# Issuing operand loads ahead of transposes, w_down sums six products later, and the cast of x three quads later

## The chip, the cores and the metric

The kernel runs on one core of one Trainium2 chip. The metric is device time in microseconds, the median of several executions.

## The reference

```python
# x: (8, 1024, 1024), w_gate, w_up: (1024, 4096), w_down: (4096, 1024), all float32
gate = x @ w_gate
up = x @ w_up
gate = 0.5 * gate * (1 + np.tanh(np.sqrt(2 / np.pi) * (gate + 0.044715 * gate ** 3)))
h = gate * up
return (h @ w_down).astype(np.float32)
```

## The kernel before

The 8192 rows of x are worked in eight passes (0 to 7) of 1024. Each pass has a gate/up phase and a down phase (the first two matrix products of the reference, and the third). Both are written with fewer block products than the plain way (sums of blocks are formed first), in a plain form for passes 0 to 2 (gate/up) and 0 to 3 (down), and in a finer, "fast" form for the rest. The fast form needs more sums of weight blocks. Those of w_gate and w_up are made in passes 1 and 2 and kept in HBM, the chip's large memory, as `w_ops`. Those of w_down are made in eight "units", two in each of the down phases of passes 2 and 3 and of the gate/up phases of passes 3 and 4, and kept as `wd_quads`. Operands are read from HBM into SBUF, the memory that the engines read, and TensorE's products are "evicted", that is read out of its accumulators by VectorE and ScalarE.

The fast gate/up phase is 8 "quads" of 26 products, so 208 products, numbered from 0. A unit there is a load followed by 20 steps, three products apart. The step number k is used all through this text. Each step first issues the stores of what the step before made, then takes the buffer that has been free longest and makes one sum on VectorE, some steps also a copy on ScalarE:

```python
def gate_up_fast(p):
    owed = {}
    steps = {}
    if p in UNITS_UP:                                   # passes 3 and 4
        free = deque(hf["s3"][:, 4096 + j * 512 : 4608 + j * 512] for j in range(8))
        for i, u in enumerate(UNITS_UP[p]):             # two units
            load, fs = wd_unit(u, hf["s3"][:, 0:4096], free)
            steps[i * 78] = load
            for k, f in enumerate(fs):
                steps[i * 78 + 14 + 3 * k] = f
    for q in range(NQ):
        # ... extra = the steps of this quad
        if q == 2 and p + 1 < NPASS:
            extra.setdefault(3, []).append(lambda: cast_x(p + 1))
        owed = quad(p, q, owed, extra)

def cast_x(p):                                          # fp32 to fp16, HBM to HBM
    r = slice(p * TOK, (p + 1) * TOK)
    nc.gpsimd.dma_start(out=xh[r, :], in_=x2[r, :])

# in wd_unit:
def stores():
    for v, n in made:
        nc.sync.dma_start(out=wdq[...], in_=v...)       # wd_quads
        if n < 8:
            free.append(v)
    made.clear()
def step(i):
    stores()
    n, op, a, b = WD_SUMS[i]
    v = at[n] = free.popleft()
    combine(node(n), op, node(a), node(b))              # VectorE
    # ... some steps also a scaled copy on ScalarE; buffers without further use are freed
```

Eight buffers serve a unit, and some are taken again four steps, 12 products, after their store.

Stores, operand loads and transposes are all issued by one engine, SyncE, in program order. And the down phase of the plain form reads w_down in chunks through a ring in SBUF:

```python
for v, name in enumerate(DSEQ):                         # 7 products of 2 chunks
    for nb in range(2):
        kc = 2 * v + nb
        for g in range(G):
            # ... 8 matmuls on chunk kc
            if v == 0 and nb == 0 and g == 0:
                flush()
            # ... evictions; the loads of two w_down units (steps 0)
            if nb == 0 and g == 0 and p + 1 < NPASS:
                if v == (2 if p < FAST - 1 else 0):     # pass 2: in the first product
                    transpose_x(p + 1)                  # four transposes on SyncE
        # p > 0:
        if kc == 0 and p < FAST:
            for k in range(3, 6):
                load_d(p, k)                            # chunks 3 to 5
        load_d(p, kc + 6)
```

Of the kernel before, what the change touches and what calls it, by code (L numbers as in the profile page):

```python
# [173 lines left out]
def kernel(  # L174
# [20 lines left out]
    NPASS = M // TOK  # L195
# [3 lines left out]
    FAST = 3  # L199
# [47 lines left out]
    def cast_x(p):  # L247
        r = slice(p * TOK, (p + 1) * TOK)
        nc.gpsimd.dma_start(out=xh[r, :], in_=x2[r, :])

    def transpose_x(p):
        for n, kh, mh in (("b11", 0, 0), ("b21", 1, 0), ("b12", 0, 1), ("b22", 1, 1)):
            r0 = p * TOK + mh * MH
            nc.sync.dma_start_transpose(  # L254
                out=xq[n], in_=xh[r0 : r0 + MH, kh * MH : (kh + 1) * MH]
            )
# [74 lines left out]
    def load_raw(p, q):  # L331
        if q < NQ:
            for w in range(2):
                nc.gpsimd.dma_start(
                    out=raw(p, q)[:, w], in_=w_v[w][:, :, q * 512 : (q + 1) * 512]
                )
# [182 lines left out]
    def d_chunk(p, k):  # L519
        if p == 0 and k % 2:  # L520
            return half_block(k // 2)
        o = 4096 * d_place(p, k)
        return rg[:, o : o + 4096].rearrange("p (n h) -> p n h", n=8)

    def load_d(p, k):
        if p >= DFAST:
            load_q(k + 2)
        elif k < 14 and (p or k % 2 == 0):
            nc.sync.dma_start(out=d_chunk(p, k), in_=wdop[k])
# [10 lines left out]
    def load_q(c):  # L540
        if c < len(WD_ENTRIES):
            nc.sync.dma_start(out=q_chunk(c), in_=wdq[c])
# [48 lines left out]
    def flush():  # L591
        for f in pending:
            f()
        pending.clear()
# [163 lines left out]
    def load_a(c):  # L758
        if c < NQ * NCH:
            q, j = divmod(c, NCH)  # L760
            nc.sync.dma_start(
                out=a_chunk(c).rearrange("p (e n) -> p e n", e=2), in_=wop[q, j]
            )
# [81 lines left out]
# [3 lines that stand above are left out]
        if p in UNITS_UP:  # L848
            free = deque(hf["s3"][:, 4096 + j * 512 : 4608 + j * 512] for j in range(8))
            for i, u in enumerate(UNITS_UP[p]):  # L850
                load, fs = wd_unit(u, hf["s3"][:, 0:4096], free)
                steps[i * 78] = load
                for k, f in enumerate(fs):
                    steps[i * 78 + 14 + 3 * k] = f
        for q in range(NQ):
            extra = {k: [steps[q * SLOTS + k]] for k in range(SLOTS) if q * SLOTS + k in steps}
            if q == NQ - 1 and p >= DFAST:
                for c in range(2):
                    extra.setdefault(2 + c, []).append(lambda c=c: load_q(c))
            if q == 2 and p + 1 < NPASS:  # L860
                extra.setdefault(3, []).append(lambda: cast_x(p + 1))
            owed = quad(p, q, owed, extra)
        for n in sorted(owed):
            pending.extend(owed[n])
# [11 lines left out]
    def down(p):  # L876
# [8 lines left out]
        def store(n, g, mh, hh):  # L885
            r0 = p * TOK + mh * MH + g * P
            nc.sync.dma_start(
                out=out2[r0 : r0 + P, hh * HH : (hh + 1) * HH], in_=tmp[:, t[n, g]]
            )
            tmp_free.append(t[n, g])  # L890

        def snap(n, g, b="a"):
            nc.scalar.activation(tl((n, g)), ps_all[:, bank[b, g]], COPY, scale=OSC)  # L893

        def add(n, b, g):
            o = tmp[:, t[n, g]]
            nc.vector.scalar_tensor_tensor(o, ps_all[:, bank[b, g]], OSC, o, MUL, ADD)

        def hsum(o, a, b, op, r):
            s = slice(4 * r, 4 * r + 4)  # L900
            nc.vector.tensor_tensor(hq[o][:, s, :], hq[a][:, s, :], hq[b][:, s, :], op)
# [41 lines left out]
        steps = {}  # L943
# [10 lines left out]
        for v, name in enumerate(DSEQ):  # L954
            b = CHAIN[name]
            first = name in ("P1", "P5")
            lhs = hq[D_OPERAND[name]]
            for nb in range(2):
                kc = 2 * v + nb
                dc = d_chunk(p, kc)  # L960
                for g in range(G):
                    if first and nb == 0:
                        bank[b, g] = ps_free.popleft()
                    for n in range(8):
                        j = 8 * nb + n
                        nc.tensor.matmul(  # L966
                            ps_all[:, bank[b, g]],
                            lhs[:, j, g * P : (g + 1) * P],
                            dc[:, n, :],
                            start=(first and j == 0),  # L970
                            stop=(j == NP - 1),
                            skip_group_check=True,
                        )
                    if v == 0 and nb == 0 and g == 0:
                        flush()
                    for f in todo:
                        f()
                    todo.clear()
                    if nb == 1:
                        if name == "P1":  # L980
                            bank["c", g] = ps_free.popleft()
                            nc.scalar.copy(ps_all[:, bank["c", g]], ps_all[:, bank["a", g]])
                        elif name == "P2":
                            snap("s1", g, "c")
                            ps_free.append(bank["c", g])
                            todo.append(lambda g=g: store("s1", g, 0, 0))
                        elif name == "P6":
                            snap("s2", g)
                        elif name == "P7":
                            snap("s3", g)  # L990
                            add("s3", "b", g)
                            todo.append(lambda g=g: store("s3", g, 1, 1))
                        elif name == "P3":
                            add("s2", "b", g)
                            ps_free.append(bank["b", g])
                            todo.append(lambda g=g: store("s2", g, 0, 1))
                        elif name == "P4":
                            snap("o21", g)
                            ps_free.append(bank["a", g])
                            todo.append(lambda g=g: store("o21", g, 1, 0))  # L1000
                    for s in sums.get((name, nb, g), ()):
                        hsum(*s)
                    for f in steps.get((2 * v + nb) * G + g, ()):
                        f()
                    if p == 0:
                        for f in half_work.get((kc, g), ()):
                            f()
                    if nb == 0 and g == 0 and p + 1 < NPASS:

                        if v == 0 and 0 < p < FAST - 1:  # L1010
                            cast_x(p + 1)
                        if v == (2 if p < FAST - 1 else 0):
                            transpose_x(p + 1)
                    if v >= x_from and work:
                        work.popleft()()
                if p == 0:
                    if kc == 0:
                        for k in (2, 4, 6):
                            load_d(p, k)
                    load_d(p, {0: 8, 6: 10, 8: 12}.get(kc, 14))  # L1020
                else:
                    if kc == 0 and p < FAST:
                        for k in range(3, 6):
                            load_d(p, k)
                    load_d(p, kc + 6)
                if p + 1 < FAST:
                    if kc == 10:
                        load_raw(p + 1, 0)
                elif p + 1 < NPASS and kc >= 8:
                    ahead = order[0]  # L1030
                    order[0] = ahead[2:] + ahead[:2]
                    load_a(2 * (kc - 8))
                    load_a(2 * (kc - 8) + 1)
                    order[0] = ahead
# [225 lines left out]
    for p in range(NPASS):  # L1260
        if p < FAST:
            gate_up_one(p)
        else:
            gate_up_fast(p)
        if p < DFAST:
            down(p)
        else:
            down_fast(p)
# [30 lines left out]
```

## Time and profile before

| | before |
|---|---|
| timed, three runs | 2276.72, 2282.41, 2283.21 us |
| profiled span | 2273.7 us |
| TensorE busy | 2255.4 us |
| down phase of pass 2, and of passes 0, 1 and 3 | 103.89, and 96.69 us |
| fast gate/up of pass 3, of pass 4, undisturbed (pass 6) | 183.77, 181.95, 181.65 us |

The prediction below shows the lines that these come from. How to read them: TensorE sets the time, and its share of busy time says only how little is left. The place of that little is found by timing equal phases against each other: a phase with the same matmuls that is longer than its sisters has lost the difference. The granted clock is the share of full TensorE clock in a stretch; the "sync queue" is what SyncE issues, in order.

### The profile page before, as it was taken

What the parts mean: (1) busy time and instruction counts of PE and PEld (TensorE: products, weight loads), DVE (VectorE), ACT (ScalarE), POOL (GpSimd) and SP (SyncE); (2) the same over time, 40 slices, a digit from 0 to 9 for tenths busy, and PEclk for the clock granted to TensorE, in tenths of its full rate; (3) what the DMA queues carried; (4) which work ended last, traced back from release to release, by engine and by line L of the source; (5) the groups of instructions that cost most, each with busy time, mean ns of one, the idle gap of its engine ahead of it and who ended that gap; (6) DMA issues with size and microseconds to landing.
All of it is one profiled execution on the core that took longest, in us unless ns stands there. A gap on an engine that the chain in (4) does not pass through costs nothing.

```text
span 2273.7 us, 42142 instructions
## 1 busy us (share of the span) xinstructions
PE 2255.4 (99%) x16255; PEld 1587.4 (70%) x16255; DVE 1522.1 (67%) x2170; ACT 959.7 (42%) x1876; POOL 688.1 (30%) x826
## 2 busy tenths in 40 slices
PE   9999999999999999999999999999999999999999
PEld 4444444444444445888458888888888888888888
DVE  5576368772587745876558777766776667866674
ACT  4443135651355522665226651255403553045620
POOL 1342013330133300554105450145402543034520
PEclk9999999999999999999999999999999999999999
DMA  9998959988799999998999999998989989988876
GB/s 231 180 207 209 260 144 217 228 248 261 177 214 225 267 300 317 326 381 291 263 356 334 372 331 305 332 307 287 304 315 323 322 273 322 313 315 275 283 289 229
DMA packets 305306, 632.98 MB, mean 278 GB/s; under 512 B 78992, under 2 KB 181392, under 8 KB 285840
## 3 DMA queue, kind: packets, MB, share of 16 engines
q1 hardware_dynamic: 250048, 556.88, 71.7%
q0 software_dynamic: 55056, 73.41, 19.4%
q8 instruction: 127, 2.08, 0.4%
q14 instruction: 75, 0.61, 0.1%
HBM read 565.18 MB, written 138.41 MB: 309 GB/s over the span
## 4 chain that ended last, share of the span: by engine, by line
PE 94%; DMA 3%; DVE 2%; issue 0%; SPq 0%; ACT 0%; DVEq 0%; ACTq 0%
PE ps L827 37%; PE ps L620 23%; PE ps L966 17%; PE ps L1080 16%; DMA ring<-w_ops 2%; DMA h_s<-wd_ops 1%; PE ps L1179 1%; DVE ring L349 1%; DMA h_a<-in_x_dram 0%; DMA ring<-wd_ops 0%; DVE x_sums L277 0%; SPq L254 0%; DVE tmp L639 0%; DVE h_a L657 0%; DVE h_s L410 0%
## 5 line engine op out<-in xcount | busy, mean ns | idle before, releaser
L827 PEld LDWEIGHTS <-ring 128*128 128x128 f16 x8320 | 813.6, 98 | 97.5 <-issue 2.5
L804 POOL TENSOR_TENSOR h_a<-tmp 128x256 f16<-128x256 f32 x640 | 471.8, 756 | 787.2 <-ACT tmp L792 774.4
L827 PE MATMUL ps<-x_sums,ring 128*128 128x256 f16 x5760 | 656.2, 273 | 0.3 <-DVE tmp L789 0.2
L789 DVE TENSOR_TENSOR tmp<-tmp,ps 128x512 f32<-128x512 f32 x640 | 414.3, 682 | 146.5 <-PE ps L827 102.9
L620 PEld LDWEIGHTS <-ring 128*128 128x128 f16 x2632 | 257.2, 98 | 314.0 <-issue 3.9
L774 ACT COPY tmp<-ps 128x512 f32<-128x512 f32 x520 | 303.2, 584 | 219.7 <-PE ps L827 142.0
L620 PE MATMUL ps<-x_sums,ring 128*128 128x512 f16 x1504 | 341.0, 379 | 2.2 <-DVE ring L349 1.7
L792 ACT ACTIVATE tmp<-tmp 128x256 f32<-128x256 f32 x640 | 263.2, 417 | 175.6 <-DVE tmp L787 81.6
L966 PE MATMUL ps<-ring,h_a 128*128 128x512 f16 x1408 | 307.3, 381 | 5.4 <-DMA ring<-wd_ops 5.4
L827 PE MATMUL ps<-x_b,ring 128*128 128x256 f16 x2560 | 306.0, 273 | 1.5 <-DVE tmp L789 1.3
L966 PEld LDWEIGHTS <-h_a 128*128 128x128 f16 x1536 | 150.5, 98 | 188.0 <-issue 7.9
L646 POOL TENSOR_TENSOR h_a<-tmp 128x512 f16<-128x512 f32 x94 | 150.1, 1596 | 374.8 <-ACT tmp L644 276.4
L787 DVE TENSOR_TENSOR tmp<-ps,tmp 128x512 f32<-128x512 f32 x240 | 165.3, 689 | 144.2 <-ACT tmp L774 98.8
L620 PE MATMUL ps<-x_b,ring 128*128 128x512 f16 x1128 | 259.2, 379 | 0.0
L639 DVE TENSOR_TENSOR tmp<-ps,tmp 128x512 f32<-128x512 f32 x188 | 127.0, 683 | 138.1 <-ACT tmp L631 135.3
L1080 PEld LDWEIGHTS <-h_a 128*128 128x128 f16 x1792 | 175.3, 98 | 20.4
L1080 PE MATMUL ps<-ring,h_a 128*128 128x256 f16 x1536 | 172.9, 273 | 0.0
L1137 ACT ACTIVATE tmp<-ps 128x512 f32<-128x512 f32 x48 | 28.2, 597 | 290.1 <-PE ps L1080 219.7
L631 ACT COPY tmp<-ps 128x512 f32<-128x512 f32 x188 | 109.9, 585 | 92.1 <-PE ps L620 89.5
L893 ACT ACTIVATE tmp<-ps 128x512 f32<-128x512 f32 x64 | 37.9, 596 | 240.1 <-PE ps L966 240.1
L349 DVE TENSOR_TENSOR ring<-ring 128x1024 f16<-128x1024 f16 x188 | 132.7, 720 | 5.8 <-PE ps L966 3.8
L644 ACT ACTIVATE tmp<-tmp 128x512 f32<-128x512 f32 x94 | 58.8, 626 | 146.4 <-DVE tmp L639 146.4
(94 smaller groups left out, 1552.6 us busy)
## 6 DMA issues: line engine op xcount, KB each, us to landing
ring<-w_ops SPq DMA_DIRECT2D x480, 512.0 KB, 5.2
ring<-wd_quads SPq DMA_DIRECT2D x88, 1024.0 KB, 6.2
ring<-wd_ops SPq DMA_DIRECT2D x49, 1024.0 KB, 7.2
out_dram<-tmp SPq DMA_DIRECT2D x128, 256.0 KB, 6.2
w_ops<-x_sums SPq DMA_DIRECT2D x110, 256.0 KB, 6.4
ring<-in_w_gate_dram POOLq DMA_DIRECT2D x23, 1024.0 KB, 9.2
ring<-in_w_up_dram POOLq DMA_DIRECT2D x23, 1024.0 KB, 17.9
w_ops<-h_s SPq DMA_DIRECT2D x82, 256.0 KB, 5.3
```

The lines of the kernel that those rows point to most:

```text
L349: nc.vector.tensor_tensor(o, a, b, op)
L620: nc.tensor.matmul(ps(b, w), lhs[:, k], rhs[:, k, :], start=(first and k == 0), stop=(k == KH - 1), skip_group_check=True,)
L639: nc.vector.tensor_tensor(o, ps("b", w), o, ADD)
L646: nc.gpsimd.tensor_tensor(hq[TO[n]][:, i, :], tmp[:, t[n, 1]], tmp[:, t[n, 0]], MUL)
L774: nc.scalar.copy(tmp[:, t[o[1]]], ps_all[:, bank[o[2]]])
L787: nc.vector.tensor_tensor(d, b, a, SUB)
L789: nc.vector.tensor_tensor(d, a, b, ADD if o[4] == "add" else SUB)
L792: nc.scalar.activation(d, d, GELU, scale=GSC)
L804: nc.gpsimd.tensor_tensor(h, tmp[:, t[o[1]], MQ : 2 * MQ], g, MUL)
L827: nc.tensor.matmul(ps_all[:, bank[c], w * MQ : (w + 1) * MQ], lhs[:, w, k], rhs[:, k], start=(first and w == 0 and k == 0), stop=(k == KH ...
L966: nc.tensor.matmul(ps_all[:, bank[b, g]], lhs[:, j, g * P : (g + 1) * P], dc[:, n, :], start=(first and j == 0), stop=(j == NP - 1), skip_ ...
L1080: nc.tensor.matmul(ps_all[:, bank[c], m * MQ : (m + 1) * MQ], lhs[:, j, m * P : (m + 1) * P], rhs[:, j, :], start=(first and j == 0 and m ...
```

## The change

It is meant to take two waits off TensorE's path: that of pass 2's down phase for chunk 3, by issuing chunks 3 to 5 ahead of the transposes, and those of the gate/up phases of passes 3 and 4 for a unit's load, by starting the steps later and moving the cast away from that load.

```diff
                 for k, f in enumerate(fs):
-                    steps[i * 78 + 14 + 3 * k] = f
+                    steps[i * 78 + 20 + 3 * k] = f
...
-            if q == 2 and p + 1 < NPASS:
+            if q == 5 and p + 1 < NPASS:
                 extra.setdefault(3, []).append(lambda: cast_x(p + 1))
...
                     if v == 0 and nb == 0 and g == 0:
                         flush()
+                        if p < FAST:
+                            for k in range(3, 6) if p else (2, 4, 6):
+                                load_d(p, k)
...
-                if p == 0:
-                    if kc == 0:
-                        for k in (2, 4, 6):
-                            load_d(p, k)
-                    load_d(p, {0: 8, 6: 10, 8: 12}.get(kc, 14))
-                else:
-                    if kc == 0 and p < FAST:
-                        for k in range(3, 6):
-                            load_d(p, k)
-                    load_d(p, kc + 6)
+                load_d(p, kc + 6 if p else {0: 8, 6: 10, 8: 12}.get(kc, 14))
```

## The prediction

> **What bounds the kernel now.** I read the page first (busy shares), then the chain of waits in order of time, then the time of each phase as stretches between the chain's turning points, then the sync queue's own timeline in the stretches that are too long. The page says that TensorE is busy 2255.4 of 2273.7 us, so at most 18.3 us can come from waits that end (a little more where a wait also slowed the clock), and whatever does not shorten TensorE's path is free.
>
> ```profile
> PE 2255.4 (99%) x16255; PEld 1587.4 (70%) x16255; DVE 1522.1 (67%) x2170; ACT 959.7 (42%) x1876; POOL 688.1 (30%) x826
> ```
>
> ```profile
> PE ps L966 <- DMA ring<-wd_ops: 5.4, 1, 5.4
> ```
>
> ```profile
> 795.30 13.83 PE ps L966 x64
> ...
> 814.84 6.54 DMA ring<-wd_ops
> ...
> 821.42 77.77 PE ps L966 x352
> 899.19 54.16 PE ps L827 x496
> ...
> 953.36 14.40 DMA ring<-w_ops
> ...
> 975.54 8.29 DMA h_s<-wd_ops
> ```
>
> The second line, from TensorE's waits (total, times, longest), is the largest of TensorE, a single one: in the down phase of pass 2 it stands 5.4 us for an operand chunk. The chain (start, length, what) leaves TensorE there, and again in the gate/up phases of passes 3 and 4, where it runs through slow operand loads (w_ops) into the load of a w_down unit (h_s from wd_ops).
>
> The next view sums stretches, one phase each: the down phases of passes 0, 1, 2 and 3, then the fast gate/up phases of passes 3, 4 and 6.
>
> ```profile
> 214.08:310.77 96.69, 96.69 (x449) 43.80 (x448) 46.88 (x50) 11.76 (x20) 5.67 (x5) 1.00 0.90 236
> 505.10:601.80 96.70, 96.70 (x450) 43.83 (x448) 37.10 (x43) 11.87 (x20) 4.44 (x5) 1.00 0.84 228
> 795.14:899.19 104.05, 98.65 (x451) 44.31 (x450) 53.45 (x87) 18.56 (x32) 3.41 (x4) 0.98 1.00 305
> 1082.96:1179.65 96.69, 96.69 (x450) 43.85 (x449) 55.34 (x88) 19.21 (x35) 7.37 (x8) 1.00 1.05 304
> 899.19:1082.96 183.77, 182.13 (x1665) 162.67 (x1664) 133.75 (x228) 110.75 (x242) 92.57 (x126) 1.00 0.95 332
> 1179.65:1361.60 181.95, 181.81 (x1666) 162.73 (x1665) 134.83 (x228) 110.88 (x242) 92.08 (x126) 1.00 0.98 348
> 1452.43:1634.08 181.65, 181.65 (x1666) 162.73 (x1665) 121.13 (x191) 106.31 (x229) 88.12 (x125) 1.00 0.90 308
> ```
>
> After the stretch come its length, then TensorE's busy time. The same 448 matmuls take 96.69 us in three down phases and 104.05 in pass 2: 7.36 too long. The fast gate/up takes 181.65 undisturbed, 183.77 in pass 3 (2.12 too long), 181.95 in pass 4 (0.30). These three excesses, 9.78 us, are all that the change can reach.
>
> Why the chunk was late is in the sync queue's timeline, and the stall in pass 3 in ScalarE's and TensorE's:
>
> ```profile
> 795.37 3.52 SPq L470 DMA_DIRECT2D x_sums<-wd_ops  x6
> 798.99 15.75 SPq L254 DMA_TRANSPOSE x_b<-x_half  x4
> 814.84 3.14 SPq L529 DMA_DIRECT2D ring<-wd_ops  x5
> ```
>
> ```profile
> 983.85 0.63 ACT L500 ACTIVATE h_s<-h_s 128x512 f16<-128x512 f16 x1 [3.90 <-DMA h_s<-wd_ops]
> ```
>
> ```profile
> 983.47 1.03 PE L827 MATMUL ps<-x_b,ring 128*128 128x256 f16 x8 [1.32 <-DVE tmp L789]
> ```
>
> The ring's chunks 3 to 7 were issued at 814.84, only after four transposes had held the queue for 15.75 us. TensorE had finished its first three chunks by 795.14 + 3 x 6.91 = 815.87. In pass 3 ScalarE stood 3.9 us for the unit's load. VectorE then evicted late, and TensorE waited for it.
>
> **What the Trainium skill says.** (1) "DMA: Bandwidth & Descriptors", section "Anatomy of one DMA — SWDGE (gpsimd) path": a DMA's semaphore wait is done by the issuing sequencer before dispatch, not by the DMA engines. So a DMA behind a held one in the same queue waits too; the trace agrees (15.75 us of transposes ahead of the loads). (2) Same page, "Issuing engines are not separate DMA queues": transfers of sync and gpsimd interleave on the same 16 engines. The trace agrees: after the cast of x was issued by gpsimd at 947.22, a w_ops load took 14.40 us, against a median of 5.2. (3) "TensorE: Matmul & The Clock Gate", section "What's actually happening": an array idle for about 3.4 us or more falls to half clock and needs about as long of work to come back. The trace agrees: after the 5.40 us wait the granted clock was 0.75 from 821.42 to 828, and ten matmuls took 3.95 us where they are normally 0.216 apart (96.69/448). So the wait costs 7.36 - 5.40 = 1.96 us beyond its length.
>
> **The change part by part.** It adds and removes no arithmetic: the same instructions stand on each engine, and only the sync and gpsimd queues and the places of some VectorE and ScalarE steps change.
>
> (a) Loads ahead of the transposes. In passes 0 and 1 nothing but the place in the program changes: the instruction order of the sync queue is the same there, as the transposes are issued only in the third product there. In pass 2 the three loads of chunks 3 to 5 move ahead of the six unit loads and four transposes. Their ring slots were last read by the gate/up matmuls, which end at about 795.1, so they can be issued at about 795.4 instead of 814.84. Three chunks of 1 MB at the stretch's better rate, 400 GB/s (418 right after the stall), take some 8 us: chunk 3 should land by about 801 to 803, 13 us before it is needed (815.87), chunks 4 and 5 by 807. The wait of 5.40 and the slow clock of 1.96 both go: -7.36 us.
>
> (b) Unit steps of the gate/up six products later. A product is 181.65/208 = 0.873 us, so the steps start 6 x 0.873 = 5.2 us later. In pass 3 ScalarE asked at 983.85 - 3.90 = 979.95. It will ask at 985.2, after the old landing at 983.83. That alone removes the 2.12 and the 0.30.
>
> (c) The cast in the sixth quad: 3 x 26 x 0.873 = 68 us later. In pass 3 it goes from 947 to about 1015, in pass 4 from 1228 to about 1296. That is clear of the second unit's load at product 78 (about 967), so this load no longer stands behind a blocked sync queue. It is also in time: 2 MB landed in 15.6 us, and the transposes come at 1083. Parts b and c aim at the same 2.42 us and each would nearly do alone.
>
> Sum: -7.36 - 2.42 = -9.78. From this I take back about 0.8, for the second rival below.
>
> **The rivals.** First, the queue is only reordered: chunks 6 and 7 and the stores to wd_quads stay behind the transposes, and these now start behind 3 MB more. They begin at about 803, and take 16 to 22 us (15.75 here, 22.29 in pass 3's down phase), so chunk 6 is issued at 819 to 825 and lands 7 to 10 us later, at 826 to 835. TensorE wants it at 795.14 + 6 x 6.91 = 836.6. That holds, by 2 to 10 us. If it fails, or if the late stores hold ScalarE's snapshots, a new wait on the ring of 2 to 5 us stands at the seventh chunk and the gain falls to some 4 us. Chance about one in eight.
>
> Second, the cast now meets the middle of the second unit. It comes after product 5 x 26 + 3 = 133, behind step 11 of that unit (98 + 3 x 11 = 131), where before it came after product 55, behind step 13 of the first unit (14 + 3 x 13 = 53). Stores to wd_quads issued in the next 15 us land late, and by the program's order of buffers some are wanted again four steps (10 us) after their store with VectorE waiting in order. Before, the sync queue stood for some 8 us after the cast (no issue from 954.65 to 963.00) and TensorE had no wait there, which speaks for slack. A repeat two steps earlier could cost 0 to 2 us in each of passes 3 and 4. I count 0.8 in all.
>
> Third, nothing moves: if the timed runs are ruled by something that this profile doesn't show, the gain drowns. The three timed runs spread from 2276.72 to 2283.21, while the profiled run took 2275.76. The spread of 6.5 us is nearly the size of the gain. It may be the very stalls that the change removes (they hang on the DMA's load), and then the change gives more than 9.
>
> A loss of 2% (46 us) would need TensorE idle for many times what any of these give. A gain of 2% is out of reach with 18.3 us of idle time and 2 of slow clock.
>
> **Range and chances.** 2282.4 - 9.0 = 2273.4 us, -0.4%. The profiled span should be near 2273.7 - 9.0 = 2264.7. Low end: all 9.8 won and the timed runs at the fast end of before, 2276.7 - 9.8 = 2267, less some luck: 2264. High end: 4 won from 2283.2, plus a little: 2281. The chance of faster by over 2% is 0.01, of within 2% 0.98, of slower by over 2% 0.01.
>
> **What would show it.** In pass 2 the down phase should last 96.7 us with no TensorE wait on the ring and the granted clock at 1.00 (step a); the three loads should be issued before the transposes, at about 795. The gate/up phases of passes 3 and 4 should be 181.7 to 182.5 (steps b, c), with no ScalarE wait on h_s from wd_ops. Passes 0, 1 and 5 to 7 should be unchanged. A wait of TensorE on the ring near the seventh chunk would prove the first rival, a wait on VectorE near the sixth quad of passes 3 or 4, behind a store to wd_quads, the second. If the phases shrink and the timed median doesn't, the third holds.

## More of the kernel before

"Step k's store" is the one that step k issues, of what step k - 1 made. Following the queue of free buffers by hand gives, for both units, that steps 14 to 17 write the buffers of the stores of steps 10 to 13, so step 16 that of step 12 and step 17 that of step 13: four steps, 12 products.

## The result, and the profile after

| | before | after |
|---|---|---|
| timed median (4 runs each) | 2280.80 us | 2279.63 us |
| lowest and highest | 2276.72, 2283.21 | 2276.39, 2280.80 |
| profiled span | 2273.7 us | 2274.6 us |

The ratio is 0.9994, with a 95% interval from 0.9975 to 1.0014. Ratios here are the mean time of one kernel's fast runs over that of the other's of the same rounds, so not quite the ratio of the medians. The change moved nothing that can be told from noise. The phases tell another story. First the stretches of the changed kernel: down phase of pass 2, then the fast gate/up of passes 3, 4 and 6 (stretch, its length, TensorE's busy time, then the other engines, the granted clock, the DMA's share and GB/s).

```profile
795.79:892.48 96.69, 96.69 (x450) 43.88 (x449) 53.48 (x87) 18.32 (x32) 3.42 (x4) 1.00 1.04 326
...
892.48:1079.32 186.84, 183.22 (x1666) 163.48 (x1664) 134.98 (x227) 112.61 (x242) 92.37 (x126) 0.99 0.95 328
1176.01:1362.50 186.49, 183.35 (x1667) 163.53 (x1665) 136.08 (x228) 112.54 (x242) 92.02 (x126) 0.99 0.98 338
1453.32:1634.98 181.66, 181.66 (x1667) 162.82 (x1665) 121.17 (x191) 106.32 (x229) 88.22 (x125) 1.00 0.90 308
```

Pass 2's down phase won its 103.89 - 96.69 = 7.20 us. But gate/up of pass 3 is now 186.84 - 181.65 = 5.19 us too long (2.12 before) and that of pass 4 is 4.84 too long (0.30 before): 10.03 us lost, 7.61 more than before. The gain was real, and was given back in two other phases. In pass 6, which holds no unit, the cast was moved as well and costs nothing (181.65 before, 181.66 now).

The issues of the sync queue in pass 2 (start, length, what; the count at the end) show the first part done as meant: chunks 3 to 5 go out at 795.87, and the transposes hold the queue behind them.

```profile
795.87 1.58 SPq L529 DMA_DIRECT2D ring<-wd_ops  x3
797.50 4.56 SPq L470 DMA_DIRECT2D x_sums<-wd_ops  x6
804.54 17.16 SPq L254 DMA_TRANSPOSE x_b<-x_half  x4
821.80 1.00 SPq L529 DMA_DIRECT2D ring<-wd_ops  x2
```

Now gate/up of pass 3. First the waits of TensorE in the changed kernel (total, times, longest), then the timelines of GpSimd (the cast), of the sync queue, of VectorE and of TensorE:

```profile
PE ps L827 <- DVE tmp L789: 6.8, 2, 3.6
```

```profile
1008.63 0.59 POOL L249 DMA_DIRECT2D x_half<-in_x_dram  x1
```

```profile
1009.09 0.37 SPq L481 DMA_DIRECT2D wd_quads<-h_s  x1
1011.29 2.07 SPq L761 DMA_DIRECT2D ring<-w_ops  x2
1013.45 0.38 SPq L481 DMA_DIRECT2D wd_quads<-h_s  x1
```

```profile
1024.94 0.43 DVE L277 TENSOR_TENSOR h_s<-h_s 128x512 f16<-128x512 f16 x1 [3.49 <-DMA wd_quads<-h_s]
...
1027.77 0.43 DVE L277 TENSOR_TENSOR h_s<-h_s 128x512 f16<-128x512 f16 x1 [1.20 <-DMA wd_quads<-h_s]
```

```profile
1028.84 3.31 PE L827 MATMUL ps<-x_sums,ring 128*128 128x256 f16 x16 [3.62 <-DVE tmp L789]
```

Read upwards: TensorE stood 3.62 us for an eviction of VectorE. VectorE was late because its steps 16 (at 1024.94) and 17 (at 1027.77) each waited for a store to wd_quads to read their buffer out. Step 16 waited for step 12's store, issued at 1009.09, step 17 for step 13's, issued at 1013.45. Both were issued after the cast (1008.63). The chain of waits gives the second one as 14.23 us under way, from 1013.45 to 1027.67; from 985 to 1005 such a store took a median of 5.0. The rest of the 5.19 us is the slow clock after the wait: 183.22 - 181.65 = 1.57 us of TensorE's busy time.

So the theory after the result, the "theory of the buffers", was: a store issued within the cast's 15 us lands too late for the step that takes its buffer four steps (10.5 us) later. Before, the cast stood at the same sort of place in the first unit, but steps 12 and 13 had sent their stores ahead of it. The rivals were that the sixth quad itself is a bad place; that the later steps meet TensorE's evictions badly; and that any cast in the middle of a unit holds the sync queue and so the operands.

### The profile page after: what moved, and what is told of

It is laid out like the page before. It is cut to its first block, busy times and chain, and to the rows that moved or that the text cites. A ratio compares the mean times of both kernels' runs of the same rounds, so it can differ in the third digit from the quotient of the medians.

```text
span 2274.6 us, 42143 instructions
## 1 busy us (share of the span) xinstructions
PE 2256.0 (99%) x16255; PEld 1589.0 (70%) x16255; DVE 1527.3 (67%) x2170; ACT 963.3 (42%) x1876; POOL 687.4 (30%) x826
## 4 chain that ended last, share of the span: by engine, by line
PE 95%; DVE 3%; DMA 2%; issue 1%; ACT 0%; SPq 0%; DVEq 0%; ACTq 0%
PE ps L827 39%; PE ps L620 22%; PE ps L966 17%; PE ps L1074 16%; DMA wd_quads<-h_s 1%; DVE ring L349 1%; PE ps L1173 1%; DVE tmp L639 0%; DMA h_a<-in_x_dram 0%; DVE h_a L657 0%; DVE h_s L277 0%; DVE x_sums L277 0%; DVE tmp L789 0%; DVE h_s L410 0%; DVE h_s L414 0%
```

## The experiments

Eleven kernels were run, in five batches. All outputs are right. The first batch takes the change apart.

**The loads alone.** Steps and cast stay as before:

```diff
-                    steps[i * 78 + 20 + 3 * k] = f
+                    steps[i * 78 + 14 + 3 * k] = f
-            if q == 5 and p + 1 < NPASS:
+            if q == 2 and p + 1 < NPASS:
```

> Only the loads of chunks 3 to 5 move ahead of the transposes; unit steps and cast stay as before. All theories: the down phase of pass 2 takes 96.7 us instead of 104.05, TensorE's wait of 5.4 us on the ring is gone, and the gate/up phases of passes 3 and 4 stay at about 183.8 and 182.0. Span about 2273.7 - 7.4 = 2266.3, ratio to before about 0.997. If the gain of the loads is an accident of one run, the phase stays above 100 us.

Measured: 2271.36 us (four runs) against 2278.34 of the kernel before in the same rounds, ratio 0.9963 (0.9948 to 0.9978). The stretches are the down phase of pass 2 and gate/up of passes 3 and 4:

```profile
795.25:891.94 96.69, 96.69 (x450) 43.90 (x449) 53.64 (x87) 18.32 (x32) 3.47 (x4) 1.00 1.03 322
891.94:1075.15 183.21, 182.09 (x1666) 162.74 (x1664) 133.75 (x228) 110.75 (x242) 92.65 (x126) 1.00 0.96 336
1171.84:1357.99 186.15, 183.49 (x1667) 163.69 (x1665) 134.78 (x228) 111.09 (x242) 92.31 (x126) 0.99 0.97 338
```

The loads are worth their 7.20 us by themselves. The third line is a miss: pass 4's loss was expected at 0.3 and is 4.50, with nothing of that phase changed. Its chain runs, as before, through operand loads of 15.88 and 7.73 us behind the cast into the late load of the unit. So the wait that steps and cast were meant to remove is not fixed at 0.30 us but differs from trace to trace.

**Loads and steps, the cast back in the third quad.** Against the changed kernel:

```diff
-            if q == 5 and p + 1 < NPASS:
+            if q == 2 and p + 1 < NPASS:
```

> Loads moved and unit steps six products later, the cast back in the third quad. Theory of the buffers (a store to wd_quads issued within the cast's 15 us lands too late for the step that takes its buffer four steps on): the cast, after product 55, now stands behind step 11 of the FIRST unit (20 + 33 = 53), so the same stall as in the changed kernel comes, but in the third quad: gate/up of passes 3 and 4 at about 186.5 each, span about 2274. Rival 'the late place of the cast is at fault' (sixth quad busier): no stall, about 181.7 each, span about 2264. Rival 'the later steps meet the evictions at a worse place': about 186.5 each, but with the stall in the sixth quad as before.

Measured, one look: 2273.86 us; gate/up of pass 3 184.43 us, of pass 4 186.24. The stall moved to the third quad, behind the same kind of store; the chain of this run shows it in pass 3:

```profile
945.43 13.23 DMA wd_quads<-h_s
```

So the sixth quad is not at fault: the stall goes with the cast. Pass 3 lost 2.78 us and not 4.9, because its wait of 2.62 us did not lower the clock (1.00 from 959.84 to 965).

**Loads and cast, the steps at their old place:**

```diff
-                    steps[i * 78 + 20 + 3 * k] = f
+                    steps[i * 78 + 14 + 3 * k] = f
```

> Loads moved and cast in the sixth quad, unit steps at their old place (14). Theory of the buffers: the cast after product 133 stands behind step 13 of the second unit (92 + 39 = 131), as it stood harmlessly in the first unit of the kernel before, and the second unit's load is no longer held up: gate/up of passes 3 and 4 at about 181.7 each, span about 2273.7 - 9.8 = 2263.9, ratio 0.996. Rival 'a cast in the sixth quad costs wherever the steps stand': about 186.5 each, span about 2274, ratio 1.000.

Measured: 2266.57 us (2265.83 to 2267.48, five runs) against 2278.34, ratio 0.9944 (0.9932 to 0.9957). Gate/up of passes 3 and 4:

```profile
892.70:1074.35 181.65, 181.65 (x1665) 162.77 (x1664) 134.02 (x228) 111.12 (x242) 92.99 (x126) 1.00 0.97 340
1171.04:1352.70 181.66, 181.66 (x1667) 162.82 (x1665) 134.73 (x228) 111.04 (x242) 92.38 (x126) 1.00 0.99 348
```

No loss is left in either. The cast is in the same quad as in the changed kernel and only the steps are six products earlier. Here step 13's store left the sync queue at 1006.69 and the cast came at 1008.85, 2.2 us behind it.

**The changed kernel with the cast one quad later:**

```diff
-            if q == 5 and p + 1 < NPASS:
+            if q == 6 and p + 1 < NPASS:
```

> The changed kernel with the cast one quad later (after product 159, behind the last step at 155). Theory of the buffers: nothing of a unit is left to collide with, so 181.7 in both gate/up phases, span about 2263.9, ratio 0.996. Rival 'the later steps are at fault and not the cast': about 186.5 each, span about 2274, ratio 1.000.

Measured: 2267.05 us (2265.68 to 2267.77, five runs), ratio 0.9945 (0.9933 to 0.9958), both phases 181.65 and 181.66 us. The later steps are harmless without a cast among them. This kernel and the one before it beat both the kernel before and the change; their five runs lie within 2.1 us, where nine of the kernel before in the same rounds lie between 2276.81 and 2281.75.

The second batch tries the theory itself: the cast moved in small steps, and a further buffer.

**The cast three products later, and six:**

```diff
-                extra.setdefault(3, []).append(lambda: cast_x(p + 1))
+                extra.setdefault(6, []).append(lambda: cast_x(p + 1))   # the other run: 9
```

> The changed kernel with the cast three products later (behind product 136, between steps 12 and 13 of the second unit). Theory of the buffers: step 12's store to wd_quads goes out before the cast, step 13's still after it; step 17, which takes step 13's buffer, waits, step 16 no longer does: gate/up of passes 3 and 4 between 184 and 187 each. Rival 'any cast in the middle of a unit holds the sync queue and so the operands': the same 186.5 as in the changed kernel, and the same again with the cast three products further on.

Measured, one look: 2280.90 us, phases 188.76 and 189.15. As the theory has it, step 16 no longer waits and step 17 does:

```profile
1029.21 0.43 DVE L277 TENSOR_TENSOR h_s<-h_s 128x512 f16<-128x512 f16 x1 [6.17 <-DMA wd_quads<-h_s]
```

The wait is longer than in the changed kernel, and the phases longer than the 184 to 187 expected: the later the cast, the later its stores land.

> The changed kernel with the cast six products later (behind product 139, after step 13 of the second unit). Theory of the buffers: the stores of steps 12 and 13 are both out before the cast and no later step takes a buffer of a later store, so the stall is gone: 181.7 in both phases, span about 2264. Rival 'a cast in the middle of a unit': still about 186.5.

Measured, one look: 2282.69 us, phases 188.28 and 190.04. This is a clear miss, and looks as the rival said. The sync queue shows what was wrong with the expectation. Step 13's store, due behind product 137, stood behind two operand loads that wait for their own products, and left at 1014.74. The cast, which waits for no product, was issued at 1015.23, so only 0.5 us after it. Step 17 then waited 4.63 us for it. Places in the program of different queues do not say which is issued first.

**A ninth buffer** (1 KB per partition):

```diff
+    spare = const.tile([P, 1 * 512], FP16, name="spare")
...
-        free = deque(hf["s3"][:, 4096 + j * 512 : 4608 + j * 512] for j in range(8))
+        free = deque(
+            [hf["s3"][:, 4096 + j * 512 : 4608 + j * 512] for j in range(8)]
+            + [spare[:, j * 512 : (j + 1) * 512] for j in range(1)]
+        )
```

> The changed kernel, cast and steps where they are in it, with a ninth small buffer for the unit's sums (all that memory holds). Theory of the buffers: a buffer then comes round one step later (five steps, 13 us, instead of four, 10.5 us), so most of the 14 to 16 us of a slow store is covered: VectorE waits under 2 us a time and the phases take 182 to 183.5 each. Rivals that blame the operands' loads, the sync queue or the sixth quad: no difference, about 186.5 each.

Measured, one look: 2267.55 us, phases 181.92 and 182.28. The cast and the stores stand as in the changed kernel (1008.96, and 1013.77 for step 13's), the stores are as slow, and yet TensorE no longer waits for VectorE. Only step 17, which with nine buffers takes that of step 12's store, still waits a little:

```profile
1024.53 0.48 DVE L278 TENSOR_TENSOR h_s<-h_s 128x512 f16<-128x512 f16 x1 [1.08 <-DMA wd_quads<-h_s]
```

So it is the wait for a buffer that costs, and neither the operands nor the later steps.

The third and fourth batch mend the miss.

**The cast nine products later, and the old steps with the cast three products earlier:**

```diff
-                extra.setdefault(3, []).append(lambda: cast_x(p + 1))
+                extra.setdefault(12, []).append(lambda: cast_x(p + 1))
```

> The changed kernel with the cast nine products later. The last two runs mended the theory: what counts is not the place in the program but the time from the issue of step 13's store (held in the sync queue until 1014.7 in the run before) to the issue of the cast; 2.2 us ahead was enough in the run with the old steps, 0.5 us was not. Here the cast should be issued about 1018, some 3 us behind that store: no wait of VectorE for wd_quads, both gate/up phases at 181.7 to 182.3. Rival 'with the steps at their new place, any cast in the middle of the second unit stalls': 186 to 190 each.

Measured, one look: 2274.09 us. Gate/up of passes 3 and 4:

```profile
893.02:1074.67 181.65, 181.65 (x1666) 162.77 (x1664) 134.78 (x227) 112.62 (x242) 92.32 (x126) 1.00 0.97 341
1171.37:1360.20 188.83, 184.59 (x1666) 164.26 (x1665) 136.09 (x228) 112.38 (x242) 92.11 (x126) 0.98 0.97 334
```

The cast was not issued at 1018 but at 1014.47, again 0.5 us behind the store. Between products 139 and 142 GpSimd has no other work, so its queue, and with it the whole program, is the same as in the run six products later; the two traces have the same order of work on every engine. It is then a repeat of that run, on another chip, and shows that a lead of 0.5 us can go either way: no stall in pass 3, 7.2 us lost in pass 4.

> Unit steps at their old place, cast in the sixth quad but three products earlier than in the change (behind product 130). Mended theory: the cast is then issued ahead of step 13's store, so step 17 waits although the steps stand where they stood before: gate/up of passes 3 and 4 at 184 to 190 each. Rival 'the old place of the steps is safe': 181.7 each.

Its edit, against the changed kernel: steps at `i * 78 + 14`, cast at `extra.setdefault(0, [])`. Measured, one look: 2276.97 us, phases 186.32 and 186.75. The store of step 13 left at 1007.29, 0.5 us ahead of the cast at 1007.79 (1290.30 and 1290.59 in pass 4), not behind it as expected; step 17 waited 3.15 and 3.59 us. The old place of the steps is not safe in itself: three products less between steps and cast bring the stall back.

**The cast 14 products later,** still in the middle of the unit:

```diff
-                extra.setdefault(3, []).append(lambda: cast_x(p + 1))
+                extra.setdefault(17, []).append(lambda: cast_x(p + 1))
```

> The changed kernel with the cast 14 products later (behind product 147), still in the middle of the second unit, with the sync queue held by it as before. The last pair showed that six and nine products later are the same order on GpSimd's queue (no other work of GpSimd lies between), with the cast 0.5 us behind step 13's store, where a stall came in three of four phases. Here three products of GpSimd lie between, so the cast should be issued about 1021 to 1023, some 7 us behind the store. Theory of the buffers: no wait of VectorE for wd_quads, both gate/up phases 181.7 to 182.3, span about 2264. Rival 'with the steps at their new place, any cast in the middle of the second unit stalls': 184 to 190 each.

Measured, one look: 2267.19 us, both phases 181.65 us. The cast came at 1022.23, 8.0 us behind step 13's store (1014.22). The sync queue's gaps behind the cast are as long as ever (from 1026.84 to 1036.96 only two operand loads were issued), and TensorE has no wait. The last of the three rivals falls with this.

The runs side by side. "Lead" is the time from the issue of step 13's store to that of the cast, in passes 3 and 4, for the unit that the cast meets; negative means the cast was first. "Lost" is the phase less 181.65 us.

| kernel | lead | waits for a store | lost in pass 3, pass 4 |
|---|---|---|---|
| before (first unit) | 2.2, 2.2 | none | 2.12, 0.30 (late load) |
| loads alone (first unit) | 2.4, 2.2 | none | 1.56, 4.50 (late load) |
| changed kernel | -4.8, -4.7 | steps 16 and 17 | 5.19, 4.84 |
| loads and steps (first unit) | -4.8, -4.7 | steps 16 and 17 | 2.78, 4.59 |
| cast 3 later | -0.4, -0.3 | step 17 | 7.11, 7.50 |
| cast 6 later | 0.5, 0.5 | step 17 | 6.63, 8.39 |
| cast 9 later (same program) | 0.5, 0.5 | none; step 17 | 0.00, 7.18 |
| steps old, cast 3 earlier | 0.5, 0.3 | step 17 | 4.67, 5.10 |
| loads and cast | 2.2, 2.2 | none | 0.00, 0.01 |
| cast 14 later | 8.0, 7.7 | none | 0.00, 0.00 |
| cast one quad later (behind the unit) | 17.9, 18.0 | none | 0.00, 0.01 |
| ninth buffer | -4.8, -4.7 | step 17, 1.08 and 1.48 us | 0.27, 0.63 |
| cast in columns (below) | -4.8, -4.7 | none | 0.10, 0.19 |

With eight buffers and the cast in one piece, a lead of 0.5 us or less loses in 11 of 12 phases, and one of 2.2 us or more has no wait for a store in ten of ten. No run has a lead between the two.

**Why a store behind the cast is slow.** In the changed kernel the 16 us after the cast show this (queue, packets, MB, share of 16 engines; q0 is GpSimd's, q1 SyncE's):

```profile
q0 software_dynamic: 80, 2.10, 61.0%
q1 hardware_dynamic: 1086, 2.49, 40.3%
```

Of the cast's 80 packets 16 have 4 bytes, by the packet records of the trace, and the other 64 have 32 KB each and take a median of 2.43 us. (The expectation below spreads the bytes over all 80 and says 26 KB.) The sync queue's data packets have 1 or 4 KB. The Trainium skill, "DMA: Bandwidth & Descriptors", section "Queues, rings and completion order", says that each DMA engine takes turns between the queues it has work for, a whole packet at a time. A large packet then holds up a small one of another queue. The trace agrees, to the packet. From 1013.0 to 1021.0, with the cast on its way, the two queues started these:

```profile
q0 software_dynamic: 48, 1.57, 91.7%
q1 hardware_dynamic: 48, 0.09, 3.5%
```

Packet for packet they have equal shares, and so the sync queue moved 0.09 MB where it had moved 2.72 MB (1151 packets) from 999.0 to 1007.0. A store that is caught therefore lands when the cast does: step 12's at 1024.92, the cast at 1024.74. In all 11 phases that lost, the store first waited for landed within 1.8 us of the cast. The last run cuts the cast into columns, at its place in the change:

```diff
     def cast_x(p):
         r = slice(p * TOK, (p + 1) * TOK)
+        if p > FAST:
+            for j in range(2):
+                c = slice(j * MH, (j + 1) * MH)
+                nc.gpsimd.dma_start(out=xh[r, c], in_=x2[r, c])
+            return
         nc.gpsimd.dma_start(out=xh[r, :], in_=x2[r, :])
```

> The changed kernel with the casts of passes 4 to 7 issued at their place in it, but as two transfers of 512 columns each instead of one contiguous transfer. In the profile of the changed kernel the cast's 2.10 MB are 80 packets of 26 KB each, in whose 15 us the stores and operand loads of the sync queue take 14 to 16 us. Theory 'the few large packets make the others wait': with rows of 512 elements (1 KB written) the packets are many and small, the stores land in under 10 us and the stall of steps 16 and 17 goes: both gate/up phases under 184. Rival 'the cast's bytes, not its packets': the stores stay slow for as long, both phases at about 186.5 or longer.

Measured, one look: 2268.01 us, phases 181.75 and 181.84, no wait of VectorE for a store in either phase. Step 12's and 13's stores took 7.24 and 8.35 us in pass 3 (15.83 and 14.23 in the changed kernel). The 26 us around the cast of pass 3 now show small packets:

```profile
q1 hardware_dynamic: 2625, 5.96, 63.1%
q0 software_dynamic: 1993, 2.02, 46.5%
```

The cast itself takes longer (median 22.9 us a half, where the whole took 15.7), and the stores in that window land in a median of 11.1 us, a little over the 10 expected. But none was late for its buffer. The same bytes in small packets do no harm, as the skill's account has it. The edit by itself would not tell smaller packets from a cast that is in two pieces and spread over more time. The count of the turns does: from 1013.0 to 1021.0 the sync queue here had 554 packets and 1.53 MB, beside 710 of the cast.

## Why the prediction was right or wrong

The total was within its range, 2279.63 - 2273.4 = 6.2 us off its center in the timed median and 2274.6 - 2264.7 = 9.9 in the profiled span. That it was within is luck: the high end of 2281 was made for the first rival, with 4 us still won, and what came is a gain wholly given back for another reason. The center had the right parts and one of them, the 0.8 us of the second rival, badly mis-sized: by 10.03 - 0.8 = 9.2 us, as much as the whole gain.

- Step a, the loads ahead of the transposes (-7.36): right. The sum is 0.16 us too large, as its stretch begins 0.16 us too early (795.14); from 795.30 the phase took 103.89 us, so the excess was 7.20, of it 7.20 - 5.40 = 1.80 for the slow clock. The phase takes 96.69 us in every run with the change, the loads were issued at 795.87, predicted at about 795.4, and the loads-alone run shows the gain in the timed median too (-7.0 us). One reading went too far: the 15.75 us of transposes do not show a queue held by a semaphore. Of the sync queue's waits from 790 to 830 only 1.8 us are the transposes' for a semaphore; what took the rest is not shown.
- Rival 1, chunks 6 and 7 behind the transposes: did not come. They were issued at 821.80, inside the predicted 819 to 825, and TensorE never waited for the ring.
- Steps b and c, the unit's late load (-2.42): right that the waits go; they are in none of the runs that move the cast. "Each would nearly do alone" was half right. The cast alone does it (loads and cast). The steps alone trade the wait for a stall of the same kind as the change's.
- Rival 2, the cast in the middle of the second unit: the mechanism was right, to the four steps and the engine that waits, and also the place to look for it. The term failed: 0.8 us in all were taken back, and it cost 5.19 + 4.84 = 10.03. The reasoning behind the size is what fell: that "the sync queue stood for some 8 us after the cast (no issue from 954.65 to 963.00) and TensorE had no wait there, which speaks for slack". That quiet showed no slack in the buffers. The last store whose buffer is wanted four steps on had left 2.2 us ahead of the cast. The prediction had both numbers, step 13 then and step 11 now, and did not ask which stores stand between.
- Rival 3, the spread of the timed runs: partly right. The runs without the stalls spread over 1.7 to 2.1 us, those of the kernel before over 4.9 us. One cause is seen: the late load of pass 4 cost 0.30 us in the trace of before and 4.50 in that of the loads alone. The best versions gained about 12 us timed, while the two traces differ by 2273.7 - 2264.8 = 8.9. The profiled run of before was a lucky one: at 2275.76 us it is the fastest of its 18 runs (the others took 2276.72 to 2283.21). In the first batch the timed medians split into 2278.34 - 2271.36 = 6.98 us for the loads and 2271.36 - 2266.57 = 4.79 for the cast moved away from the late load, where the trace of before has 2.42 to win. There is no trace of the other runs, so that the late load makes up the difference is not shown.

In numbers: predicted -7.36 - 2.42 + 0.8 = -9.0; measured in the traces -7.20 - 2.42 + 10.03 = +0.41. The spans differ by +0.9; gate/up of pass 1, which took 0.54 us longer, makes up the rest.

## What to carry to other kernels

When a large transfer is moved, look for the small transfers that will now stand behind it, and ask of each who needs its end and when: a store is only off the path while its buffer is not wanted. With few buffers in turn that is a deadline a few steps on, and a small lead is no safety (here 0.5 us mostly lost and 2.2 us was enough). Three remedies worked here: one buffer more, a place for the large transfer where nothing urgent is pending, and smaller packets. And order in the program is not order of issue between queues: read the issue times of both.

## What the Trainium skill lacked or had wrong

- "DMA: Bandwidth & Descriptors", section "SWDGE vs HWDGE vs iDMA", gives packets as preferably at most 4096 B. The contiguous HBM-to-HBM cast went in 64 packets of 32 KB, and the page has no figure for what such packets do to others: stores of 128 KB took 14.23 us instead of 5.0, loads of 512 KB a median of 14.2 us instead of 5.1. Two halves by columns (1993 packets in the window shown) did not stall.
- The same page has a sequencer time for transposes of small tiles, but none for how long transposes of 512 x 512 elements hold the queue that issues them: four held it for 15.75 us (pass 2, before), 17.16 (pass 2, after) and 22.29 (pass 3, before), while one lands in a median of 5.6 us.
- "TensorE: Matmul & The Clock Gate", section "What's actually happening", gives an idle window of about 3.4 us before the clock drops. Here waits of 2.67 us (loads alone, pass 4: granted clock 0.62 in the next 4.5 us) and 2.84 us (old steps, pass 3: 0.69 in the next 5.5 us) were enough, and one of 2.62 us (loads and steps, pass 3) was not. The page's free-running window may explain why there is no sharp limit; no run shows that.
- No page says what a buffer's turn costs when its store is slow; the numbers here are 10.03 us with eight buffers and 0.27 + 0.63 = 0.90 with nine.
